# Token-major down projections, and seven block products in place of eight, in a two-layer trunk's MLPs

## The chip, the cores and the metric

One core of a Trainium2 chip runs the whole kernel. The metric is device time in microseconds (us), the median of several executions; lower is better. The engines are TensorE (matrix products; the profile shows its matmuls as PE and its loads of the stationary operand as PEld), VectorE (DVE), ScalarE (ACT), GpSimd (POOL) and SyncE (SP, which issues the loads).

## The reference

256 tokens of width 2048 go through two layers: a gated short convolution with an MLP, then latent attention with an MLP. All is float32. Every sub-layer ends in a layer norm over `alpha * x + f(x)`.

```python
D_MODEL, SEQ, D_FF = 2048, 256, 4 * 2048

def layer_norm(x, g, b):
    mu = jnp.mean(x, axis=-1, keepdims=True)
    var = jnp.mean(jnp.square(x - mu), axis=-1, keepdims=True)
    return (x - mu) * lax.rsqrt(var + LN_EPS) * g + b

def sq_relu_mlp(x, w1, w2):
    return jnp.square(jax.nn.relu(x @ w1)) @ w2

for layer in range(2):
    mix = short_conv_mixer(...) if layer == 0 else mla_mixer(...)
    h = layer_norm(ALPHA * h + mix, ln_g[layer, 0], ln_b[layer, 0])
    h = layer_norm(ALPHA * h + sq_relu_mlp(h, w1[layer], w2[layer]), ln_g[layer, 1], ln_b[layer, 1])
```

Each `w1` is 2048 x 8192 and each `w2` 8192 x 2048: 64 MB each, read once.

## The kernel before, in words

**Layout.** Activations lie with the features on the partitions: `xres` holds 16 chunks of 128 features x 256 tokens. A product has a 128x128 block of weights in the array and streams the tokens.

**Precision.** A float32 value is kept as two parts of type fp32r: `hi`, the value cast to that type, and `lo`, what is left of it. A product of two values takes three partial products: hi·hi, lo·hi and hi·lo. Activations lie as 512 columns, 256 of `hi` and 256 of `lo`, so `high` (line 133) multiplies a weight block's `hi` with all 512 and `low` (line 137) its `lo` with the first 256. This pair is called a **block** here. In a result bank the first 256 columns hold two of the partial sums and the last 256 the third; who reads the bank adds them (`whole`, `residual`). `mm_k1` (lines 151 to 153) makes three 256-wide matmuls of it, so that one sum comes out; `mm_wide` (lines 164 to 166) does the same with 258 columns, which carry the gain and the shift of a layer norm whose statistics come later.

**Weights.** All weights are one `stream` of halves: 128 partitions x 1024 columns, 512 KB. `load` (lines 110 to 113) issues a half's load on SyncE's queue into one of five `raw` buffers, casts it to `hi` on ScalarE (line 112) and makes `lo` on VectorE (line 113), in one of eight pairs of `hi`/`lo` buffers (`whl`). `take` hands out the next halves and lists the conversions of `LOOK` = 4 halves more. Which instruction an engine runs when is fixed by the framework when the kernel is built: it orders each engine's instructions by the order of the listing and by when their inputs and buffers come free. On the chip every engine runs its list in order.

**An MLP.** `mlp` goes through the 8192 hidden features in `NQ` = 8 passes of 1024. In a pass the up part computes 8 chunks of 128 hidden features (16 blocks each); `hidden` adds the partial sums, takes the squared ReLU (VectorE, line 431) and splits the result into `h` (lines 198, 199). The down part then computes, for each of the 16 chunks of output features, 8 blocks over the pass's hidden features, and `residual` adds the two halves of the bank to `xres` (line 354, two 256-wide additions; in the first pass lines 458, 459 with `alpha`). Up and down part have 128 blocks each. In the first pass the up part runs with `mm_wide` and the layer norm before it is applied on the way (`normal`); in the last pass the down part runs with `mm_k1`.

**Behind an MLP.** `Norm.count` sums values and squares over the features as the chunks come out, `stats` turns them into mean and variance through TensorE, and the next stage starts with `widen`/`wide` data. Behind the second MLP, `to_out` scales by the gain, turns the 16 chunks back to tokens on the partitions (line 707), adds mean and shift by a small product of row vectors (line 739), scales by the deviation and stores.

**PSUM.** Eight banks of 512 columns, handed out in turn by `psum`.

Of the kernel before, what the change touches and what calls it, by code (L numbers as in the profile page):

```python
# [15 lines left out]
P = 128  # L16
# [15 lines left out]
LOOK = 4  # L32
RAW, WA = 5, 8
FIRST = ((0, 2, 4, 8), (0, 4, 8))
GROUP = 3
WARM = 8
WO_G = 3
# [5 lines left out]
def trunk(ctx: ExitStack, tc: tile.TileContext, xT, vecs, w_in, w_out, w_kv, w_q, w_uk, w_uv,  # L43
          w_qn, w_qp, w_o, w1, w2, cosT, sinT, mask, ident, gb, out):
# [11 lines left out]
    units = []  # L56
    for m in range(NC):
        units += [w_in[NC + m], w_in[2 * NC + m], w_in[m]]
    units += [w_out[m] for m in range(NC)]

    def mlp_units(l):
        us = []
        for q in range(NQ):
            us += [w1[l, q * QC + m] for m in range(QC)]
            us += [w2[l, m, q] for m in range(NC)]
        return us

    units += mlp_units(0)
    units += [w_kv[m] for m in range(NK + 1)] + [w_q[m] for m in range(NK)]
    for g in range(4):  # L70
        units += [w_uk[g], w_qn[g], w_uv[g], w_qp[g]]
    units += [w_o[m] for m in range(NC)]
    units += mlp_units(1)
    stream = [u[j] for u in units for j in range(u.shape[0])]
# [25 lines left out]
    def load(i, raw=None, cuts=(0, 8)):  # L100

        if raw is None:
            raw = raws.tile([P, 1024], F32, tag="raw", name=f"raw{i}")
        hi = whl.tile([P, 8, P], F32R, tag="hi", name=f"hi{i}")
        lo = whl.tile([P, 8, P], F32R, tag="lo", name=f"lo{i}")
        ready[i] = (hi, lo)
        for b0, b1 in zip(cuts, cuts[1:]):
            at, cols = slice(b0, b1), slice(P * b0, P * b1)
            rv = raw[:, cols].rearrange("p (b c) -> p b c", c=P)
            nc.sync.dma_start(raw[:, cols], stream[i][:, cols])  # L110
            yield
            nc.scalar.copy(hi[:, at, :], rv)  # L112
            nc.vector.tensor_tensor(lo[:, at, :], rv, hi[:, at, :].bitcast(F32), ALU.subtract)  # L113
            yield

    def split_upto(n):
        while state["split"] < min(n, len(stream)):
            for _ in load(state["split"]):
                pass
            state["split"] += 1  # L120

    def take(halves=2):
        i = state["next"]
        state["next"] += halves
        split_upto(i + halves + LOOK)
        return [ready.pop(i + j) for j in range(halves)]
# [12 lines left out]
    def mm_run(wps, x, k0, k1, nk, tiles_first=False):  # L139

        order = [(k, u) for k in range(k0, k1) for u in wps]
        if tiles_first:
            order = [(k, u) for u in wps for k in range(k0, k1)]
        for k, (w, ps) in order:
            high(ps, w, k, x[:, k, :], k == 0)
            low(ps, w, k, x[:, k, :], k == nk - 1)
# [8 lines left out]
    def mm(ps, w, b0, xhl, nk):  # L155

        for k in range(nk):
            mm_k1(ps, w, b0 + k, xhl[:, k, :], k == 0, k == nk - 1)

    def mm_wide(ps, w, xd):  # L160

        for k in range(NC):
            hi, lo = (t[:, k % 8, :] for t in w[k // 8])
            nc.tensor.matmul(ps[:, :W], hi, xd[:, k, :W], start=k == 0, stop=False)  # L164
            nc.tensor.matmul(ps[:, :W], lo, xd[:, k, :W], start=False, stop=False)  # L165
            nc.tensor.matmul(ps[:, :W], hi, xd[:, k, W:], start=False, stop=k == NC - 1)  # L166

    def products(n, x, nk=NC, group=0, cuts=(), halves=True, tiles_first=False):

        ws = [(take(nk // 8), psum("ps_g")) for _ in range(group)]  # L170
        at = [0, *cuts, nk]
        if halves:
            for k0, k1 in zip(at, at[1:]):
                if ws:
                    mm_run(ws, x, k0, k1, nk, tiles_first)
        else:
            for k in range(nk if group else 0):
                for w, ps in ws:
                    mm_k1(ps, w, k, x[:, k, :], k == 0, k == nk - 1)
        yield from [ps for _, ps in ws]  # L180
        for i in range(group, n):
            w = take(nk // 8)
            ps = psum("ps_u")
            if halves:
                mm_run([(w, ps)], x, 0, nk, nk)
            else:
                mm(ps, w, 0, x, nk)
            yield ps

# [32 lines left out]
    def rsqrt(out, ve):  # L222

        s = small.tile([P, 2], F32, tag="sq", name="sq")
        nc.scalar.activation(s, ve, AF.Sqrt)
        iv = small.tile([P, 2], F32, tag="iv", name="iv")
        nc.vector.reciprocal(iv, ve)
        t = small.tile([P, 2], F32, tag="rt", name="rt")
        nc.vector.tensor_tensor(t, s, iv, ALU.mult)
        a = small.tile([P, 2], F32, tag="ra", name="ra")  # L230
# [8 lines left out]
    class Norm:  # L239
# [3 lines left out]
        def __init__(self, idx, scale):  # L243
            self.idx, self.scale, self.hurry = idx, scale, idx == 3
            self.S = act.tile([P, T], F32, tag="S", name=f"S{idx}")
            self.Q = act.tile([P, T], F32, tag="Q", name=f"Q{idx}")
            self.mu0 = act.tile([P, T], F32, tag="mu0", name=f"mu0{idx}")

# [14 lines left out]
        def count(self, m):  # L263
# [7 lines left out]
            if m < NC - 1 or not self.hurry:  # L271
                nc.vector.tensor_tensor(self.S, self.S, d, ALU.add)
                nc.vector.tensor_tensor(self.Q, self.Q, sq, ALU.add)
            else:
                self.last = (d, sq)

        def widen(self):

            self.xd = act.tile([P, NC, 2 * W], F32R, tag="a", name=f"xd{self.idx}")
            v = vec[:, C_G:C_G + 128].rearrange("p (v i m) -> p m i v", v=2, i=4)[:, :, self.idx, :]  # L280
            nc.scalar.copy(self.xd[:, :, T:W], v)
            nc.vector.tensor_tensor(self.xd[:, :, W + T:], v, self.xd[:, :, T:W].bitcast(F32), ALU.subtract)

        def wide(self, m):
            d, x, g = xres[:, m, :], self.xd[:, m, :], self.gain(m)[0]
# [3 lines left out]
        def stats(self):  # L289

            st = psum("stat")
            for j in range(2):
                for b in range(2):
                    c = st[:, 2 * j + b:2 * j + b + 1]
                    tok = slice(b * P, (b + 1) * P)
                    nc.tensor.matmul(c, (self.S, self.Q)[j][:, tok], col[:, 0:1], start=True,
                                     stop=not self.hurry)
                    if self.hurry:
                        nc.tensor.matmul(c, self.last[j][:, tok], col[:, 0:1], start=False, stop=True)
# [7 lines left out]
            return nm, ve, r  # L307

        def finish(self):
            nm, _, r = self.stats()  # L310
# [15 lines left out]
        def normal(self, m, dst=None):  # L326
# [3 lines left out]
            u = tmp.tile([P, T], F32, tag="fh", name="nu")  # L330
# [7 lines left out]
        def weighted(self, ps, f):  # L338
# [6 lines left out]
            nc.scalar.activation(f, t, AF.Identity, bias=v[:, 1:2])  # L345
# [10 lines left out]
    def summed(ln, pss, add, wide):  # L356

        for m, ps in enumerate(pss):
            add(ps, m)
            ln.count(m)  # L360
            wide(m)
# [5 lines left out]
    xhl = act.tile([P, NC, 2 * T], F32R, tag="a", name="xhl0")  # L367

    first = act.tile([P, 2 * GROUP, 1024], F32, tag="b", name="first")
    for half, cuts in enumerate(FIRST):  # L370
        pieces = [load(2 * u + half, first[:, GROUP * half + u, :], cuts) for u in range(GROUP)]
        for b0, b1 in zip(cuts, cuts[1:]):
# [4 lines left out]
            for m in range(at.start, at.stop):  # L377
                put_split(xhl[:, m, :], xres[:, m, :])
# [5 lines left out]
    z = act.tile([P, NC, 2 * T], F32R, tag="b", name="z")  # L384
    cbuf = act.tile([P, 2, 5, T + 2], F32, tag="c", name="cbuf")
    pss = products(3 * NC, xhl, group=GROUP, cuts=(2, 4, 8, 12), tiles_first=True)
    ln = Norm(0, ALPHA)
    for m in range(NC):
        parts = []
        for what in "cub":  # L390
# [3 lines left out]
            parts.append(f)  # L394
            if what == "u":
                v = cbuf[:, m % 2, 3, :]
                nc.gpsimd.memset(v[:, 0:2], 0.0)
                nc.vector.tensor_tensor(v[:, 2:], parts[0], parts[1], ALU.mult)
# [5 lines left out]
        nc.vector.tensor_tensor(y, y, parts[2], ALU.mult)  # L404
        put_split(z[:, m, :], y)
# [4 lines left out]
    ln.widen()  # L410
    summed(ln, products(NC, z), residual, ln.wide)

    def mlp(idx, ln, last):

        xhl = act.tile([P, NC, 2 * T], F32R, tag="b", name=f"xhl{idx}")
        todo = iter(range(NC))

        def normal():
            k = next(todo, None)
            if k is not None:  # L420
                ln.normal(k, xhl[:, k, :])

        for q in range(NQ):
            h = act.tile([P, QC, 2 * T], F32R, tag="c", name=f"h{idx}_{q}")
            if q == NQ - 1:
                ln = Norm(idx, None)

            def hidden(m, ps, evac):
                f = tmp.tile([P, T], F32, tag="fh", name="fh")
                evac(ps, f)  # L430
                nc.vector.scalar_tensor_tensor(f, f, 0.0, f, ALU.max, ALU.mult)  # L431
                put_split(h[:, m, :], f)

            if q == 0:
                for m in range(QC):
                    w = take()
                    ps = psum("ps_w")
                    mm_wide(ps, w, ln.xd)
                    if m == 0:
                        ln.finish()  # L440
                    hidden(m, ps, ln.weighted)
                    if m > 0:
                        normal()
            else:
                for m, ps in enumerate(products(QC, xhl)):
                    hidden(m, ps, whole)
                    if q == NQ - 1:
                        for k in range(2 * m, 2 * m + 2):
                            ln.prepare(k)
            if q == NQ - 1:  # L450
                last(ln, products(NC, h, QC, 2, halves=False))
                return ln
            pss = products(NC, h, QC, 2, (6,))
            for m, ps in enumerate(pss):
                if q == 0:
                    normal()
                    d = xres[:, m, :]
                    nc.vector.scalar_tensor_tensor(d, d, ALPHA, ps[:, T:], ALU.mult, ALU.add)
                    nc.vector.tensor_tensor(d, d, ps[:, :T], ALU.add)
                else:  # L460
                    residual(ps, m)

    def to_wide(ln, pss):
        ln.widen()
# [352 lines left out]
```

## Time and profile before

| | us |
|---|---|
| median of 3 runs | 2079.16 (2077.47 to 2081.31) |
| the profiled execution | 2080.19 |
| its span, first to last instruction | 2078.4 |
| granted TensorE clock, mean | 0.998 |
| passes of the MLPs in the trace, one of the six alike | 88.7 |
| last product of the kernel ends | 2063.4 |
| loads of weights | 512 KB each, 4.1 from issue to landing for those of the MLPs |
| bytes read | 379.20 MB, 183 GB/s over the span |

A row of the costliest groups reads: line, engine, operation, what is written and read by the program's names, shapes, number of instructions | time in which at least one of them ran, mean nanoseconds of one | idle time of the engine ahead of them, and who ended most of it. Matmuls overlap, so a matmul's duration is longer than the time until the next one starts. A row of the timeline reads: start, time covered, engine, line, operation, shapes, number of instructions merged into the row, and in brackets idle time ahead of it with what ended it.

### The profile page before, as it was taken

What the parts mean: (1) busy time and instruction counts of PE and PEld (TensorE: products, weight loads), DVE (VectorE), ACT (ScalarE), POOL (GpSimd) and SP (SyncE); (2) the same over time, 40 slices, a digit from 0 to 9 for tenths busy, and PEclk for the clock granted to TensorE, in tenths of its full rate; (3) what the DMA queues carried; (4) which work ended last, traced back from release to release, by engine and by line L of the source; (5) the groups of instructions that cost most, each with busy time, mean ns of one, the idle gap of its engine ahead of it and who ended that gap; (6) DMA issues with size and microseconds to landing.
All of it is one profiled execution on the core that took longest, in us unless ns stands there. A gap on an engine that the chain in (4) does not pass through costs nothing.

```text
span 2078.4 us, 32534 instructions
## 1 busy us (share of the span) xinstructions
PE 2068.4 (100%) x12640; PEld 1841.6 (89%) x12640; DVE 1512.2 (73%) x2490; ACT 1010.8 (49%) x1473; POOL 2.2 (0%) x21
## 2 busy tenths in 40 slices
PE   9999999999999999999999999999999999999998
PEld 8888888988888888888899998898888888888898
DVE  7667677886676767667788878788667676676776
ACT  6444445654444443444456665565444444444354
POOL 0000000000000000000000000000000000000000
PEclk9999999999999999999999999999999999999999
DMA  8555555555555556565555444556555555555551
GB/s 312 196 186 189 190 185 188 176 193 187 191 191 193 188 179 202 190 189 190 192 183 173 133 142 143 188 167 202 190 188 190 193 190 187 192 192 190 188 183 62
DMA packets 107447, 383.42 MB, mean 184 GB/s; under 512 B 11927, under 2 KB 13335, under 8 KB 107287
## 3 DMA queue, kind: packets, MB, share of 16 engines
q1 hardware_dynamic: 107148, 381.09, 56.1%
q8 instruction: 99, 1.62, 0.3%
q14 instruction: 56, 0.45, 0.1%
q10 hardware_dynamic: 144, 0.26, 0.0%
HBM read 379.20 MB, written 2.10 MB: 183 GB/s over the span
## 4 chain that ended last, share of the span: by engine, by line
PE 98%; DVE 1%; DMA 0%; ACT 0%; issue 0%; DVEq 0%; ACTq 0%
PE ps_u L133 51%; PE ps_u L137 25%; PE ps_g L133 3%; PE ps_w L166 2%; PE ps_w L164 2%; PE ps_w L165 2%; PE ps_g L137 1%; PE ps_u L152 1%; PE ps_u L151 1%; PE ps_u L153 1%; PE S L612 0%; DMA xres<-in_xT_dram 0%; PE S L611 0%; PE ps_q L153 0%; PE ps_q L152 0%; PE ps_q L151 0%
## 5 line engine op out<-in xcount | busy, mean ns | idle before, releaser
L112 ACT CAST hi<-raw 128x1024 fp32r<-128x1024 f32 x712 | 747.7, 1053 | 909.1 <-PE ps_u L133 775.6
L113 DVE TENSOR_TENSOR lo<-raw,hi 128x1024 fp32r<-128x1024 f32 x712 | 870.4, 1224 | 366.6 <-ACT hi L112 344.0
L133 PE MATMUL ps_u<-xhl,hi 128*128 128x512 f32 x2512 | 874.8, 394 | 0.0
L137 PE MATMUL ps_u<-xhl,lo 128*128 128x256 f32 x2512 | 698.0, 278 | 0.0
L133 PEld LDWEIGHTS ps_u<-xhl,hi 128*128 128x128 f32 x2512 | 471.1, 188 | 110.1
L133 PE MATMUL ps_u<-h,hi 128*128 128x512 f32 x1568 | 544.2, 394 | 0.0
L137 PEld LDWEIGHTS ps_u<-xhl,lo 128*128 128x128 f32 x2512 | 472.2, 188 | 0.1
L137 PE MATMUL ps_u<-h,lo 128*128 128x256 f32 x1568 | 434.3, 277 | 0.0
L133 PEld LDWEIGHTS ps_u<-h,hi 128*128 128x128 f32 x1568 | 294.0, 188 | 68.3
L137 PEld LDWEIGHTS ps_u<-h,lo 128*128 128x128 f32 x1568 | 294.3, 188 | 0.0
L354 DVE TENSOR_TENSOR xres<-xres,ps_u 128x256 f32<-128x256 f32 x422 | 177.2, 420 | 116.2 <-PE ps_u L137 99.9
L166 PE MATMUL ps_w<-xd,hi 128*128 128x258 f32 x400 | 113.3, 284 | 0.0
L164 PE MATMUL ps_w<-xd,hi 128*128 128x258 f32 x400 | 113.2, 283 | 0.0
L165 PE MATMUL ps_w<-xd,lo 128*128 128x258 f32 x400 | 112.9, 282 | 0.0
L133 PE MATMUL ps_u<-z,hi 128*128 128x512 f32 x256 | 90.6, 399 | 0.0
L133 PE MATMUL ps_g<-h,hi 128*128 128x512 f32 x224 | 78.3, 394 | 0.0
L164 PEld LDWEIGHTS ps_w<-xd,hi 128*128 128x128 f32 x400 | 76.3, 191 | 0.1
L166 PEld LDWEIGHTS ps_w<-xd,hi 128*128 128x128 f32 x400 | 75.7, 190 | 0.0
L165 PEld LDWEIGHTS ps_w<-xd,lo 128*128 128x128 f32 x400 | 75.2, 188 | 0.0
L133 PE MATMUL ps_u<-oT,hi 128*128 128x512 f32 x208 | 73.5, 399 | 0.0
L137 PE MATMUL ps_u<-z,lo 128*128 128x256 f32 x256 | 71.7, 281 | 0.0
L198 ACT CAST h<-fh 128x256 fp32r<-128x256 f32 x128 | 51.5, 402 | 36.6 <-DVE fh L431 36.6
(211 smaller groups left out, 2091.2 us busy)
## 6 DMA issues: line engine op xcount, KB each, us to landing
raw<-in_w_dram SPq DMA_DIRECT2D x512, 512.0 KB, 4.1
raw<-in_w_in_dram SPq DMA_DIRECT2D x90, 512.0 KB, 3.4
raw<-in_w_out_dram SPq DMA_DIRECT2D x32, 512.0 KB, 3.3
raw<-in_w_o_dram SPq DMA_DIRECT2D x32, 512.0 KB, 3.4
raw<-in_w_kv_dram SPq DMA_DIRECT2D x10, 512.0 KB, 4.2
raw<-in_w_q_dram SPq DMA_DIRECT2D x8, 512.0 KB, 3.4
raw<-in_w_uk_dram SPq DMA_DIRECT2D x8, 512.0 KB, 3.3
raw<-in_w_qn_dram SPq DMA_DIRECT2D x8, 512.0 KB, 3.3
```

The lines of the kernel that those rows point to most:

```text
L112: nc.scalar.copy(hi[:, at, :], rv)
L113: nc.vector.tensor_tensor(lo[:, at, :], rv, hi[:, at, :].bitcast(F32), ALU.subtract)
L133: nc.tensor.matmul(ps, w[blk // 8][0][:, blk % 8, :], x, start=first, stop=False)
L137: nc.tensor.matmul(ps[:, :T], w[blk // 8][1][:, blk % 8, :], x[:, :T], start=False, stop=last)
L151: nc.tensor.matmul(ps[:, :T], lo, x[:, :T], start=first, stop=False)
L152: nc.tensor.matmul(ps[:, :T], hi, x[:, T:], start=False, stop=False)
L153: nc.tensor.matmul(ps[:, :T], hi, x[:, :T], start=False, stop=last)
L164: nc.tensor.matmul(ps[:, :W], hi, xd[:, k, :W], start=k == 0, stop=False)
L165: nc.tensor.matmul(ps[:, :W], lo, xd[:, k, :W], start=False, stop=False)
L166: nc.tensor.matmul(ps[:, :W], hi, xd[:, k, W:], start=False, stop=k == NC - 1)
L198: nc.scalar.copy(dst[:, :T], src)
L354: nc.vector.tensor_tensor(d, d, ps[:, :T], ALU.add)
```

## The change

All down projections of both MLPs change sides: the split activations stay in the array (128 hidden features x 128 tokens), and 512 columns of weights stream (`dot`, three matmuls of 512: hi·hi, hi·lo, lo·hi). A result bank then holds 128 tokens x 512 output features, complete; `put` adds it to a new accumulator `acc` (two token halves x 2048). A plain down projection goes through four column blocks `n` of 512 (`down`), each with two token halves `t` and 8 hidden chunks: 64 dots a pass.

In the six passes `FAST` = 1 to 6 of each MLP, the first two column blocks come from `down_fast`. For each pair of hidden chunks (1 and 2) the two token halves, the two hidden chunks and the two column blocks make a 2x2 by 2x2 product of blocks, which is done with seven products in place of eight, by sums and differences of the blocks (Strassen's scheme in Winograd's form). Four pairs make 28 dots instead of 32. The seven results stay in seven banks over the four pairs and are merged into `acc` behind them. The sums of the weight blocks are made in `prepare` on VectorE from two raw halves and converted (one unit: three pairs of hi/lo buffers, and a buffer of its own, `t4`, for the fourth difference); those of the activations in `hidden`.

At the end of the first MLP the accumulator is turned back to features on the partitions with 32 transposes, and the next stage's first three wide products run around the last of them. At the end of the second MLP the residual is turned to tokens first, and the last norm is taken along the free axis. `LOOK` becomes 5, with a unit counted as 3. The squared ReLU goes to ScalarE as a ReLU and a square. Large tiles are cut in two (`a1`, `a2`) and buffers `fh` become three.

```diff
-LOOK = 4
+LOOK = 5
+NB = 4
+BW = D // NB
+FAST = range(1, NQ - 1)
+TAIL = 4
...
+    def prepare(i):
+        if len(stream[i]) == 1:
+            raw = load_raw(i, stream[i][0])
+            hi, lo = ready[i] = parts(i)
+            split(hi, lo, tiled(raw))
+            return
+        r1, r2 = (load_raw(f"{i}_{j}", src) for j, src in enumerate(stream[i]))
+        out = []
+        def finished(r, name):
+            hi, lo = parts(name)
+            split(hi, lo, tiled(r))
+            out.append((hi, lo))
+        b22, (b21, b12) = r1[:, BW:], (r2[:, :BW], r2[:, BW:])
+        finished(r1, f"{i}_1")
+        t = raws.tile([P, 1024], F32, tag="raw", name=f"raw{i}_t")
+        two = "p (a c) -> p a c"
+        nc.vector.tensor_tensor(t.rearrange(two, a=2), b12.unsqueeze(1).to_broadcast([P, 2, BW]),
+                                r1.rearrange(two, a=2), ALU.subtract)
+        finished(t, f"{i}_t")
+        nc.vector.tensor_tensor(b12, b22, t[:, :BW], ALU.subtract)
+        finished(r2, f"{i}_2")
+        t4 = r1[:, :BW]
+        nc.vector.tensor_tensor(t4, b21, b12, ALU.subtract)
+        f = state["fast"].tile([P, 2, BW], F32R, tag="t4", name=f"t4_{i}")
+        split(f[:, 0, :], f[:, 1, :], t4)
...
+    def size(i):
+        return 1 if len(stream[i]) == 1 else 3
     def take(halves=2):
         i = state["next"]
         state["next"] += halves
-        split_upto(i + halves + LOOK)
+        ahead = -sum(size(j) for j in range(i, i + halves))
+        for j in range(i, len(stream)):
+            ahead += size(j)
+            if ahead > LOOK:
+                break
+            if j >= state["split"]:
+                prepare(j)
+                state["split"] = j + 1
...
+    def dot(ps, w, x, first, last):
+        nc.tensor.matmul(ps, x[0], w[0], start=first, stop=False)
+        nc.tensor.matmul(ps, x[0], w[1], start=False, stop=False)
+        nc.tensor.matmul(ps, x[1], w[0], start=False, stop=last)
...
+    FACTORS = (("4", "22", "T4"), ("2", "12", "21"), ("3", "S4", "22"), ("1", "11", "11"),
+               ("6", "S2", "T2"), ("7", "S3", "T3"), ("5", "S1", "T1"))
+    def down_fast(x, forms):
+        ps = {p: psum(f"ps_f{p}") for p, _, _ in FACTORS}
+        n = len(x) // 2
+        for j in range(n):
+            b, = take(1)
+            a = {"11": held(x[2 * j], 0), "12": held(x[2 * j + 1], 0), "22": held(x[2 * j + 1], 1)}
+            for i in range(4):
+                a[f"S{i + 1}"] = [forms[:, j, o, i * P:(i + 1) * P] for o in range(2)]
+            for p, l, r in FACTORS:
+                dot(ps[p], b[r], a[l], j == 0, j == n - 1)
+        return ps
...
+                if not func:
+                    nc.scalar.activation(f, f, AF.Relu)
+                nc.scalar.activation(f, f, AF.Square)
+                put_split(h[m], f)
...
+                    nc.vector.tensor_tensor(s1, a21, a22, ALU.add)
+                    nc.vector.tensor_tensor(s3, a21, a11, ALU.subtract)
+                    nc.vector.tensor_tensor(s2, s1, a11, ALU.subtract)
+                    nc.vector.tensor_tensor(s4, a12, s2, ALU.subtract)
+                    split(forms[:, m // 2, 0, :], forms[:, m // 2, 1, :], sf.rearrange("p i c -> p (i c)"))
...
+            def put(n, t, ps):
+                if q == 0:
+                    nc.scalar.copy(block(n, t), ps)
+                    for _ in range(2):
+                        normal()
+                else:
+                    nc.vector.tensor_tensor(block(n, t), block(n, t), ps, ALU.add)
...
+            if q in FAST:
+                p = down_fast(h, forms)
+                put(0, 1, p["4"])
+                put(0, 0, p["2"])
+                put(1, 0, p["3"])
+                v, u = (raws.tile([P, 2, BW], F32, tag="raw", name="vu")[:, i, :] for i in range(2))
+                put(0, 0, p["1"])
+                nc.scalar.copy(v, p["1"])
+                nc.vector.tensor_tensor(v, v, p["6"], ALU.add)
+                nc.vector.tensor_tensor(u, v, p["7"], ALU.add)
+                put(1, 0, v)
+                put(0, 1, u)
+                put(1, 0, p["5"])
+                put(1, 1, u)
+                put(1, 1, p["5"])
+            for n in range(2 if q in FAST else 0, NB):
+                down(h, put, n)
...
+    def to_wide(block, put, down):
+        def turned(n):
+            for c in range(2):
+                ps = psum("turned")
+                for j in range(4):
+                    src = block(n, j % 2)[:, (2 * c + j // 2) * P:(2 * c + j // 2 + 1) * P]
+                    nc.tensor.transpose(ps[:, j * P:(j + 1) * P], src, id_t)
+                summed(ln, [ps[:, j * T:(j + 1) * T] for j in range(2)], add, 4 * n + 2 * c)
+        ln.widen("b")
+        for n in range(NB):
+            down(put, n)
+            if n:
+                turned(n - 1)
+        ln.ws = group_of(GROUP)
+        mm_wide(ln.ws, ln.xd, 0, NC - 4)
+        turned(NB - 1)
+        mm_wide(ln.ws, ln.xd, NC - 4)
...
+    def to_out(block, put, down):
+        gbt = act.tile([P, NB, 2 * BW], F32, tag="b", name="gbt")
+        for n in range(NB):
+            nc.gpsimd.dma_start(gbt[:, n, :], gb[n].partition_broadcast(P))
...
+        def finished(n, t, ps):
+            put(n, t, ps)
+            nc.vector.bn_stats(out=stats[:, t, n, :], in_=block(n, t))
+            if n < NB - 1:
+                return
...
+            rsqrt(r, ve)
+            for i in range(NB):
+                d, u = block(i, t), raws.tile([P, 1024], F32, tag="raw", name="u")[:, :BW]
+                nc.vector.scalar_tensor_tensor(u, d, mv[:, 0:1], gbt[:, i, :BW], ALU.subtract, ALU.mult)
+                nc.vector.scalar_tensor_tensor(d, u, r, gbt[:, i, BW:], ALU.mult, ALU.add)
+                nc.sync.dma_start(out[t * P:(t + 1) * P, i * BW:(i + 1) * BW], d)
+        for n in range(NB):
+            down(finished, n, TAIL if n == NB - 1 else 0)
```

On the host, `w2` is laid out as rows of 512 columns for two hidden chunks to a half, and once more (`w2f`) in the order of the pairs for the fast passes; each weight is still loaded once.

423 lines of the change are left out of this document (206 added, 217 removed).

## The prediction

> **What bounds the kernel now.** I read the page from the top: busy shares, then the chain that ended last, then the costliest groups; then the waits, one pass by itself, and single instructions where the change needs a price.
>
> ```profile
> PE 2068.4 (100%) x12640; PEld 1841.6 (89%) x12640; DVE 1512.2 (73%) x2490; ACT 1010.8 (49%) x1473; POOL 2.2 (0%) x21
> ...
> PE 98%; DVE 1%; DMA 0%; ACT 0%; issue 0%; DVEq 0%; ACTq 0%
> ...
> L112 ACT CAST hi<-raw 128x1024 fp32r<-128x1024 f32 x712 | 747.7, 1053 | 909.1 <-PE ps_u L133 775.6
> L113 DVE TENSOR_TENSOR lo<-raw,hi 128x1024 fp32r<-128x1024 f32 x712 | 870.4, 1224 | 366.6 <-ACT hi L112 344.0
> L133 PE MATMUL ps_u<-xhl,hi 128*128 128x512 f32 x2512 | 874.8, 394 | 0.0
> L137 PE MATMUL ps_u<-xhl,lo 128*128 128x256 f32 x2512 | 698.0, 278 | 0.0
> ```
>
> TensorE is the bound: 98% of the chain, and no idle time before its groups. VectorE has a quarter of the span free. What ScalarE's casts wait for (775.6 us) is TensorE giving back converted weights: the conversion runs as far ahead as the eight hi/lo buffers let it, although the listing asks for four halves (LOOK). Counting both sequences, a half in the fourth pass is converted 17 us before its first use. So the order of the listing is a priority, not the order on the engines.
>
> One pass of the first MLP, of the six that look alike:
>
> ```profile
> core 0: us, PE busy (x) PEld busy (x) DVE busy (x) ACT busy (x) POOL busy (x), PEclk, DMA share, GB/s
> ...
> 549.50:638.20 88.70, 88.70 (x513) 77.55 (x513) 60.88 (x89) 38.30 (x48) 0.00 (x0) 1.00 0.59 190
> ```
>
> TensorE is full for 88.7 us, VectorE works 60.9 of them. A pass is 256 blocks (128 up, 128 down), so a block, one 512-wide and one 256-wide matmul, costs 0.3465 us.
>
> **The price of the new form.** The new products hold the activations in the array and stream 512 weight columns, three matmuls to a product. The attention's value projection already does just that (lines 590 to 592; start, duration):
>
> ```profile
> 1149.40 0.40 PE L590 MATMUL ps_v<-hi,lat 128*128 128x512 f32 x1
> 1149.64 0.39 PE L591 MATMUL ps_v<-lo,lat 128*128 128x512 f32 x1
> 1149.87 0.39 PE L592 MATMUL ps_v<-hi,lat 128*128 128x512 f32 x1
> 1150.10 0.39 PE L590 MATMUL ps_v<-hi,lat 128*128 128x512 f32 x1
> 1150.32 0.39 PE L591 MATMUL ps_v<-lo,lat 128*128 128x512 f32 x1
> 1150.55 0.39 PE L592 MATMUL ps_v<-hi,lat 128*128 128x512 f32 x1
> 1150.78 0.39 PE L590 MATMUL ps_v<-hi,lat 128*128 128x512 f32 x1
> ```
>
> Starts, not durations, are the price, since matmuls overlap: six in 1.38 us, 0.230 each; later ones of the run come every 0.227. A product costs 0.680 to 0.690; I take 0.685. It replaces two blocks, 0.693. The upper bound for the same work is 0.696, twice the sum of the median spacings of the block's two forms in the whole trace (0.231 and 0.117).
>
> **TensorE's part of the sum.**
> - A down projection is 64 such products, or 28 + 32 = 60 in the twelve fast passes. Before, 128 x 0.3465 = 44.35 us; fast, 60 x 0.685 = 41.10. Saved 3.25 x 12 = 39.0.
> - The two first passes keep 64 products: 43.84, saved 0.5 x 2 = 1.0.
> - The two last passes ran three 256-wide matmuls a block (lines 151 to 153, started every 0.120 us): 128 x 0.361 = 46.2. Now 43.84, saved 2.4 x 2 = 4.7.
> - The first MLP's result now lies with tokens on the partitions and is turned back: 32 transposes at 0.108 us (the start spacing of line 707's): +3.5. The second MLP's 32 replace 32.
> - Together -41.2. With 0.680 a product it is -46, with 0.696 -30.
>
> **The end.** Before, the last product ended at 2063.4 and the span at 2078.4: 15 us of statistics, row products, scaling and stores. After, the last token half does an addition (0.69), statistics of 512 elements (about 0.7), some eight small operations (0.16 to 0.20 each in this tail), four pairs of 512-wide operations and a store (2.4 us from issue to landing): about 11 us, behind the first token half's same work, of which some 2 us stick out behind the 5.5 us of its last products. 13 us, -2. Bounds: -5 if nothing sticks out and the store is short, +4 if the first half's work comes wholly first.
>
> **VectorE's and ScalarE's part.** What one 1024-wide conversion costs here is in the groups above, and the 512-wide row of the start gives the half size:
>
> ```profile
> 18.22 1.90 DVE L113 TENSOR_TENSOR lo<-first,hi 128x512 fp32r<-128x512 f32 x3
> ...
> 616.05 1.23 DVE L113 TENSOR_TENSOR lo<-raw,hi 128x1024 fp32r<-128x1024 f32 x1
> 617.81 0.88 DVE L354 TENSOR_TENSOR xres<-xres,ps_u 128x256 f32<-128x256 f32 x2 [0.54 <-PE ps_u L137]
> ```
>
> Three 512-wide take 1.90 us with 0.69 for the last: one starts each 0.60. Likewise 1.14 for 1024 (median spacing of line 113's when another follows), 0.34 for 256 independent and 0.45 dependent; 128 worked out as 0.20 to 0.31.
> A fast unit (one pair of loads, seven products, 7 x 0.685 = 4.8 us of TensorE) needs on VectorE three low parts and one 1024-wide difference, 4 x 1.14, and two 512-wide differences and a low part, 3 x 0.60: 6.36 us. ScalarE: 3 x 1.05 + 0.62 = 3.8, below TensorE's. So **inside the fast stage VectorE is slower than TensorE by 1.5 us a unit**, four units long. New too: the sums of the activations, 1.6 us to each of four pairs, and eleven 512-wide additions where the seven results are merged (6.6 us), instead of 16 of 256 (line 354). The square of the ReLU goes to ScalarE.
> A whole fast pass for VectorE: 24 plain halves 27.4, four units 25.4, hidden tiles 8 x 0.8, sums 6.4, fifteen additions 9: 74.6 us out of 44.35 + 41.1 = 85.5. Over a pass it fits; the question is how far ahead it can get before the stage.
>
> Ledger of the stage, 0 being the first product of the first unit. Eight hi/lo pairs: while the last up chunk holds two, three belong to unit 0 and three to unit 1. The up stage leaves VectorE idle (10 halves 11.4, seven hidden tiles and three sums 10.4, units 0 and 1 12.1: 34 of 44), so at 0 both are converted, all but unit 1's T4, whose one buffer is free when the first product of unit 0 has ended (0.9). From 0.5 VectorE has: last hidden tile 0.8, last sums 1.6, T4 of unit 1 0.6, and of unit 2 what is left behind its first low part, 5.2: ready at 8.7, wanted at 9.6. Unit 3 takes 6.36 more: 15.1, wanted at 14.4. **Late by 0.7**. The casts between (1.05) and the one T4 buffer make it wait in places where nothing else is ready; I take 1.5 us a pass, **+18 in all**. Lower bound 0, since TensorE can't run ahead of its rows. Upper bound: only one unit is ahead, unit 1 is ready at 0.5 + 2.4 + 6.36 = 9.3, unit 3 two units later at 22.0 instead of 14.4: 7.6 a pass, +91.
> While ScalarE's cast of T4 waits for TensorE, the casts behind it on ScalarE wait, and for these VectorE's low parts: that is how a small delay of T4 can become one of a whole unit.
> Behind the stage the first plain product needs two banks, and the second is that of product 4, whose addition may stand behind five conversions (5.7 us): 15.1 + 5.7 + 0.6 = 21.4 against 20.0 + 0.7. It is covered by loads that land later than that, or costs 0.7 a pass; within the 1.5.
> What is left costs nothing: the three wide units taken together run the same matmuls; the first passes' additions become ScalarE copies of 0.62 in an engine half idle; the four broadcast loads of gains go out on POOL's queue, which issues little else, some 40 us ahead of their use, and would cost their landing (about 4 us) at the end if they came late.
> Loads: the same bytes, eight halves in 20 us at the stage, some 210 GB/s against the 190 of a pass now at a DMA share of 0.59. Nothing, and if raw buffers (five, three to a unit) come free late, it is the upper bound above.
>
> By the Trainium skill, page "VectorE: DVE Perf Modes", section Terms, every operation of the engine drains its pipe before the next may issue, which speaks against an edit that adds so many. By that rule an operation would cost its whole duration, and the sum would be that of the second rival. The trace disagrees where operations are independent: 0.60 between starts for a duration of 0.69.
>
> **Sum.** The profiled execution took 2080.19 (span 2078.4 and 1.8 around it), 1.0 above the median of 2079.16. 2079.2 - 41.2 - 2 + 18 = **2054**.
>
> **Rivals.**
> 1. *TensorE alone decides.* The conversion keeps up, and the product costs 0.680 to 0.690: 2079 - 43 = 2036, down to 2031 with 0.680. For it: 12% of VectorE left in the pass. Against: 6.36 over 4.8 in the stage.
> 2. *Full durations.* 6.96 a unit (4 x 1.224 + 3 x 0.688), and unit 3 is late by about 2.3 instead of 0.7: 12 x 2.3 = 28, 2064. Against: the spacing above.
> 3. *Slower: one unit ahead.* LOOK of 5 lists one unit of size 3, five raw buffers hold two, T4 one; if the engines' fixed order keeps to that, each unit waits for VectorE. It decides from 43 / 12 = 3.6 us a pass. At the bound 2036 + 91 = 2127; at half way between 3.6 and 7.6, 2036 + 67 = 2103. Against: conversions that today run 17 us ahead.
> 4. *Even.* The stall is 3.3 to 3.9 us a pass, 2075 to 2083.
>
> **Chances.** Forecast 0.42 (its own range 2044 to 2072), rival 1 0.13, 2 0.07, 3 0.30, 4 0.08. Under 0.2%, some 4 us, a measurement of this kernel can't tell a change from none (its three runs span 3.8 us). Faster 0.62, same 0.08, slower 0.30. The range goes from 2034 to 2112: of rival 1 the lower third and of rival 3 the upper third stay outside, about 0.14.
>
> **What would show it.** The page: about 11,240 matmuls instead of 12,640, DVE near 85%, PE idle of 10 to 30 us in all, in front of the products with T4. A fast pass 85 to 88.7 us long. Starts of the new products 0.227 to 0.232 apart. If units 1, 2 and 3 each begin with a wait on T4's low part of 2 us or more, rival 3 holds; if a product costs over 0.70, the first term is wrong.

## The result, and the profile after

The changed kernel takes **2055.84 us** (median of 4 runs, 2055.07 to 2056.39) against 2078.31 for the kernel before in the same comparison: a ratio of 0.9884, 95% interval 0.9872 to 0.9896. The forecast was 2054 and faster. The profiled execution took 2055.07 us with a span of 2053.3; 2080.19 and 2078.4 before, so 25.1 us went.

The page, busy shares, chain by engine, then groups:

```profile
PE 2033.1 (99%) x11220; PEld 1761.9 (86%) x11220; DVE 1638.2 (80%) x2555; ACT 1184.8 (58%) x1847; POOL 4.5 (0%) x25
...
PE 97%; DVE 2%; DMA 0%; issue 0%; ACT 0%; DVEq 0%
...
L113 DVE TENSOR_TENSOR lo<-raw,hi 128x1024 fp32r<-128x1024 f32 x712 | 862.2, 1222 | 315.1 <-ACT hi L112 310.5
L112 ACT CAST hi<-raw 128x1024 fp32r<-128x1024 f32 x712 | 742.0, 1049 | 538.5 <-PE ps_u L191 295.3
...
L248 PE MATMUL ps_d<-hi,h 128*128 128x512 f32 x640 | 249.3, 390 | 0.0
```

TensorE is still the bound, with 1420 matmuls fewer; VectorE went from 73% to 80% of the span, not to the 85% forecast (in the fast pass below it is busy for 74.9 of 86.5 us). The third pass of the first MLP, up part, the stage of the seven products, and the plain down products; columns as before:

```profile
547.26:592.47 45.21, 45.21 (x258) 39.23 (x256) 38.06 (x59) 29.17 (x49) 0.00 (x0) 1.00 0.54 175
592.47:612.00 19.53, 19.53 (x87) 15.86 (x86) 18.07 (x24) 13.10 (x18) 0.00 (x0) 1.00 0.57 181
612.00:633.77 21.77, 21.77 (x97) 17.98 (x96) 18.81 (x23) 10.73 (x12) 0.00 (x0) 1.00 0.76 262
```

TensorE has no idle time in any of them. The pass is 86.5 us instead of 88.75. The down part is 41.3 us instead of 44.4. **The up part, whose matmuls nobody touched, is 45.2 instead of 44.4.** That is the first surprise. The second is that the wait forecast in the stage does not exist, though VectorE is full there (18.07 of 19.53):

```profile
586.95 1.22 DVE L155 TENSOR_TENSOR raw_t<-raw,raw 128x1024 f32<-128x1024 f32 x1
...
590.56 0.68 DVE L158 TENSOR_TENSOR raw<-raw,raw_t 128x512 f32<-128x512 f32 x1
...
592.95 0.69 DVE L161 TENSOR_TENSOR raw<-raw 128x512 f32<-128x512 f32 x1
593.63 1.23 DVE L113 TENSOR_TENSOR lo_t<-raw_t,hi_t 128x1024 fp32r<-128x1024 f32 x1
594.77 0.42 DVE L301 TENSOR_TENSOR fh<-ps_u,t 128x256 f32<-128x256 f32 x1
595.11 0.68 DVE L113 TENSOR_TENSOR t<-raw,t 128x512 fp32r<-128x512 f32 x1
...
599.46 0.68 DVE L113 TENSOR_TENSOR t<-raw,t 128x512 fp32r<-128x512 f32 x1
...
605.80 0.68 DVE L113 TENSOR_TENSOR t<-raw,t 128x512 fp32r<-128x512 f32 x1
```

The rows `t<-raw,t` are the low parts of T4, the last piece of units 1, 2 and 3. They end at 595.8, 600.1 and 606.5. The stage began at 592.47 and TensorE needs a unit each 4.88 us, at 597.35, 602.2 and 607.1. So VectorE is ahead by 1.5, 2.1 and **0.6 us**; over all twelve passes the smallest lead at unit 3 is 0.60. The first two rows shown are the 1024-wide difference of unit 2 and its first 512-wide one, both done before the stage begins.

Where the 25.1 us come from, stage by stage (differences of the starts of the stages' first matmuls in the two traces):

| | us |
|---|---|
| twelve fast down parts, 44.37 to 41.31 | -36.8 |
| twelve up parts of the same passes, 44.37 to 45.21 | +10.1 |
| two first down parts, 44.4 to 43.55 | -1.7 |
| last down parts with their transposes | -1.0 |
| attention up to its output projection, of it 2.85 in one wait (experiment e8) | +4.6 |
| its output projection, 73.5 to 72.1 | -1.4 |
| end, 14.9 to 13.5 | -1.4 |
| rest (start, convolution, first and last up parts) | +2.4 |

### The profile page after: what moved, and what is told of

The parts are those of the page before. It is cut to its first block, busy times and chain, and to the rows that moved or that the text cites. A ratio compares the mean times of both kernels' runs of the same rounds, so it can differ in the third digit from the quotient of the medians.

```text
span 2053.3 us, 30156 instructions
## 1 busy us (share of the span) xinstructions
PE 2033.1 (99%) x11220; PEld 1761.9 (86%) x11220; DVE 1638.2 (80%) x2555; ACT 1184.8 (58%) x1847; POOL 4.5 (0%) x25
## 4 chain that ended last, share of the span: by engine, by line
PE 97%; DVE 2%; DMA 0%; issue 0%; ACT 0%; DVEq 0%
PE ps_u L191 34%; PE ps_u L195 17%; PE ps_d L250 7%; PE ps_d L249 7%; PE ps_d L248 7%; PE ps_f L250 4%; PE ps_f L248 4%; PE ps_f L249 4%; PE ps_w L225 1%; PE ps_w L223 1%; PE ps_w L224 1%; PE ps_g L223 1%; PE ps_g L225 1%; PE ps_g L224 1%; PE ps_wo L191 1%; PE S L781 1%
## 5 line engine op out<-in xcount | busy, mean ns | idle before, releaser
L191 PE MATMUL ps_u<-xhl,hi 128*128 128x512 f32 x1792 | 632.9, 398 | 0.0
L195 PE MATMUL ps_u<-xhl,lo 128*128 128x256 f32 x1792 | 503.1, 281 | 0.0
L191 PEld LDWEIGHTS ps_u<-xhl,hi 128*128 128x128 f32 x1792 | 336.6, 188 | 83.1
L191 PE MATMUL ps_u<-xhl_a,hi 128*128 128x512 f32 x720 | 253.5, 396 | 0.0
L248 PE MATMUL ps_d<-hi,h 128*128 128x512 f32 x640 | 249.3, 390 | 0.0
L250 PE MATMUL ps_d<-hi,h 128*128 128x512 f32 x640 | 249.3, 390 | 0.0
L249 PE MATMUL ps_d<-lo,h 128*128 128x512 f32 x640 | 249.2, 389 | 0.0
L195 PE MATMUL ps_u<-xhl_a,lo 128*128 128x256 f32 x720 | 203.0, 282 | 0.0
L191 PEld LDWEIGHTS ps_u<-xhl_a,hi 128*128 128x128 f32 x720 | 135.3, 188 | 32.0
L248 PEld LDWEIGHTS ps_d<-hi,h 128*128 128x128 f32 x640 | 120.2, 188 | 25.2
L250 PEld LDWEIGHTS ps_d<-hi,h 128*128 128x128 f32 x640 | 120.1, 188 | 25.0
L195 PEld LDWEIGHTS ps_u<-xhl_a,lo 128*128 128x128 f32 x720 | 135.8, 189 | 0.0
L191 PE MATMUL ps_u<-z,hi 128*128 128x512 f32 x256 | 90.6, 399 | 0.0
```

The source lines that it names most:

```text
L191: nc.tensor.matmul(ps, w[blk // 8][0][:, blk % 8, :], x, start=first, stop=False)
L195: nc.tensor.matmul(ps[:, :T], w[blk // 8][1][:, blk % 8, :], x[:, :T], start=False, stop=last)
L248: nc.tensor.matmul(ps, x[0], w[0], start=first, stop=False)
L249: nc.tensor.matmul(ps, x[0], w[1], start=False, stop=False)
L250: nc.tensor.matmul(ps, x[1], w[0], start=False, stop=last)
```

## Experiments

Each is an edit of the changed kernel unless said. Ratios are to the kernel before in the same comparison, with the 95% interval.

**e1_plain: the form without the seven products.**

```diff
-FAST = range(1, NQ - 1)
+FAST = range(0)
```

> All down projections as plain products, 64 to a pass, no pass with seven. Compared with the changed kernel (2055.8 us) each of twelve passes has four more products, 43.5 instead of 41.3 us for its down part. Theory A (the up blocks' slower rhythm, 0.3533 us a block instead of 0.3467, is set by the products that run before them): up stages stay at 45.2 us, time 2055.8 + 12 x 2.25 = 2083 us. Theory B (it comes from VectorE's and ScalarE's added work in the pass): up stages go back to 44.4 us, time 2073 us. If the stage of the seven products hid a wait, the time falls below both.

Measured: 2081.0 us, ratio 1.0006 (0.9996 to 1.0015). All twelve up parts stay at 45.21 us although VectorE has nothing new to do in them (it is busy for 23.8 us of a stretch of 45, against 27.8 in the kernel before and 34.7 in the changed one); the down parts are 43.58. Theory B falls for VectorE. ScalarE keeps its added square here, so for ScalarE it falls only with e6 below. And the new form alone is worth nothing: 0.8 us a pass won in the down part, 0.84 lost in the up part. The gain of the change is that of the seven products.

**e2_nudge, e3_swap, e6_mu: disturbing the entry of the up part.** The edits, in this order:

```diff
+                if q in FAST:
+                    nc.tensor.matmul(psum("nudge")[:, :P], ones, ones, start=True, stop=True)
                 for m, ps in enumerate(products(QC, xhl)):
```

```diff
+            if swap and k == 1:
+                low(ps, w, k, x[k], False)
+                high(ps, w, k, x[k], False)
+                continue
             high(ps, w, k, x[k], k == 0)
...
-                for m, ps in enumerate(products(QC, xhl)):
+                for m, ps in enumerate(products(QC, xhl, swap=q in FAST)):
```

```diff
+                if q in FAST:
+                    nc.tensor.matmul(psum("nudge")[:, :T], ones, xres[:, 0, :], start=True, stop=True)
                 for m, ps in enumerate(products(QC, xhl)):
```

> The changed kernel with one 128x128 float32 matmul of ones into a bank of its own ahead of the up part of each of the twelve fast passes. Theory A (rhythm by entry): the up stages fall from 45.2 to 44.4 us, less about 0.2 us for the added matmul, 2055.8 - 12 x 0.6 = 2048 us. Theory B (load on SBUF by the other engines): up stages stay at 45.2 us, 2058 us.

> The changed kernel with the two matmuls of the second block of each fast pass's up part in the other order, no work added. Theory A: one disturbance at the entry is enough to move the whole stage into the other rhythm, 45.2 to 44.4 us, 2046 us; it may also stay if this disturbance is not of the right size. Theory B: 2056 us.

> The changed kernel with one 256-wide float32 matmul (of the kind that the norm's first mean uses, 0.43 us) into a bank of its own ahead of the up part of each of the twelve fast passes. In the last passes, where such a matmul stands there anyway, the up part runs at 0.3467 us a block. Theory A (rhythm by entry, of the right kind): up stages 45.2 to 44.4 us, together with the added matmul 2055 - 12 x 0.4 = 2050 us. If the entry is not it, up stages stay at 45.2 and the time is 2060 us.

Measured: e2 2057.2 us, ratio 0.9889 (0.9874 to 0.9903), up parts 45.30; e3 2055.92, 0.9887 (0.9872 to 0.9902), up parts 45.20. In neither does the rhythm change; e2 pays for its added matmuls. **e6: 2050.2 us, 0.9853 (0.9838 to 0.9868)**, and all twelve up parts take 44.57. The entry in the changed kernel, from its timeline, and in e6:

```profile
547.03 0.39 PE L250 MATMUL ps_d<-hi,h 128*128 128x512 f32 x1
547.26 0.39 PE L191 MATMUL ps_u<-xhl,hi 128*128 128x512 f32 x1
547.48 0.28 PE L195 MATMUL ps_u<-xhl,lo 128*128 128x256 f32 x1
547.60 0.40 PE L191 MATMUL ps_u<-xhl,hi 128*128 128x512 f32 x1
547.83 0.28 PE L195 MATMUL ps_u<-xhl,lo 128*128 128x256 f32 x1
547.95 0.40 PE L191 MATMUL ps_u<-xhl,hi 128*128 128x512 f32 x1
548.19 0.28 PE L195 MATMUL ps_u<-xhl,lo 128*128 128x256 f32 x1
548.31 0.40 PE L191 MATMUL ps_u<-xhl,hi 128*128 128x512 f32 x1
```

```profile
547.07 0.59 PE L580 MATMUL nudge<-xres,ones 128*128 128x256 f32 x2
547.31 0.59 PE L191 MATMUL ps_u<-xhl,hi 128*128 128x512 f32 x1
547.74 0.28 PE L195 MATMUL ps_u<-xhl,lo 128*128 128x256 f32 x1
547.86 0.39 PE L191 MATMUL ps_u<-xhl,hi 128*128 128x512 f32 x1
548.09 0.28 PE L195 MATMUL ps_u<-xhl,lo 128*128 128x256 f32 x1
548.20 0.39 PE L191 MATMUL ps_u<-xhl,hi 128*128 128x512 f32 x1
548.43 0.28 PE L195 MATMUL ps_u<-xhl,lo 128*128 128x256 f32 x1
548.55 0.39 PE L191 MATMUL ps_u<-xhl,hi 128*128 128x512 f32 x1
```

Read the starts of the 512-wide rows. In the changed kernel they come every 0.35 to 0.36 us, in e6 every 0.34 to 0.35. To the nanosecond, the spacings in the changed kernel repeat as 113, 233, 117, 241, 120, 236 (1060 for three blocks, 353.3 each), in e6 as 230, 117, 230, 117, 230, 116 (1040, 346.7 each). The instructions of the stage and their data are the same. The added matmul takes a result bank, so the stage's banks move on by one; in e2 they do so too, without effect. The rhythm that is taken at the entry lasts here for the 256 matmuls of the stage. The two profiled executions are 4.9 us apart (the medians 5.6). Of these 3.7 lie in the twelve passes, 0.3 each: 0.64 won in the up part, the rest paid at the added matmul and behind it. Another 1.3 lie ahead of the attention's output projection, where one wait is 0.68 instead of 2.85 in this build and other places are longer. e6 is the fastest version run; its interval against the kernel before lies below the changed kernel's.

**e10_more_mu, e11_before_mu: more such entries, and in the kernel before.** e10 adds the same matmul ahead of the second MLP's last up part and of the convolution's output projection; e11 puts it into the kernel before, ahead of the two output projections (shown):

```diff
+    def nudge():
+        nc.tensor.matmul(psum("nudge")[:, :T], ones, xres[:, 0, :], start=True, stop=True)
...
+    nudge()
     summed(ln, products(NC, z), residual, ln.wide)
...
+        nudge()
         yield from products(NC - WO_G, oT)
```

> The changed kernel with the 256-wide float32 matmul ahead of the up parts of all passes but the first, and ahead of the convolution's output projection. Theory A (entry sets the rhythm): the second MLP's last up part falls from 45.2 to 44.6 us and the output projection from 90.6 to 89.0, so 2050.2 - 0.2 - 1.2 = 2049 us. If the output projection does not follow, 2050 us.

> The kernel before, with such a matmul ahead of the convolution's output projection (90.6 us there) and of the attention's (73.5 us, 0.3533 us a block). Theory A: 89.0 and 72.1 us, 2079 - 1.6 - 1.4 + 0.9 = 2077 us. Rival: in that kernel the rhythm has another cause, stages unchanged, 2080 us.

Measured: e10 2052.62 us, 0.9868 (0.9854 to 0.9881): the last up part falls to 44.57 as expected, the convolution's output projection stays at 90.64, and the attention's, which nothing was put ahead of, goes from 72.1 to 73.5, 1.4 of the 2.6 us above the expected 2050. e11 2079.87 us, 0.9998 (0.9989 to 1.0007): the convolution's output projection falls from 90.58 to 88.94, and the attention's runs at 346.7 ns a pair instead of 353.3, though the time is at the rival's number and can't be told from that of the kernel before. Only the attention's stage is switched at its entry. The convolution's stage in the kernel before begins at 346.7 anyway; it changes to 353.3 at its 16th block (282.3 us), where TensorE has to wait a moment for the last chunk of its input `z`, and two 512-wide matmuls follow each other. With the added matmul the stage starts 0.8 us later, and this place is gone. So both rhythms occur in both kernels, and an added matmul can switch them, but the same one does it in one place and not in another.

**e4_t_twice, e12_t_three, e7_t_four: more VectorE work in each unit.** The 1024-wide difference is made two, three or four times:

```diff
-        nc.vector.tensor_tensor(t.rearrange(two, a=2), b12.unsqueeze(1).to_broadcast([P, 2, BW]),
-                                r1.rearrange(two, a=2), ALU.subtract)
+        for _ in range(2):
+            nc.vector.tensor_tensor(t.rearrange(two, a=2), b12.unsqueeze(1).to_broadcast([P, 2, BW]),
+                                    r1.rearrange(two, a=2), ALU.subtract)
```

> The changed kernel with the 1024-wide difference of every fast unit made twice: 1.14 us more of VectorE to a unit, nothing else. Theory C (the conversion keeps just ahead: by the trace the low part of T4 of unit 3 is there 0.6 us before its use, of unit 1 1.5 and of unit 2 2.1): unit 3 comes late by 1.7 to 2.8 us in every fast pass, 2076 to 2090 us, with the wait in front of the products with T4. Rival D (VectorE has room, the conversions move ahead into the up stage): 2056 to 2061 us.

> The changed kernel with the 1024-wide difference of every fast unit made four times: 3.4 us more of VectorE to a unit, 13.7 to a fast pass, which then has about 88 us of VectorE against 86.5 of TensorE. Theory F (room over the whole pass decides, since conversions and products both move): a fast pass becomes VectorE's 88 to 90 us, 2055 + 12 x 1.5 to 3.5 = 2073 to 2097 us. Theory C (the stage decides): unit 2 and 3 late by about 8 us together in every fast pass, 2140 us and more.

> The changed kernel with the 1024-wide difference of every fast unit made three times: 9.1 us more of VectorE to a fast pass. Two times (4.6 us) cost 2 us in all, four times (13.7 us) 122 us, 10.1 a pass. Theory G (a fast pass absorbs about 4 us of VectorE by running conversions ahead and ready products first, and what goes beyond comes out in full): 9.1 - 4 = 5 us a pass, 2055 + 60 = 2115 us. Rival F (only the sum over the pass counts, 83.7 us of VectorE under 86.5 of TensorE): 2056 to 2062 us.

| | VectorE added to a pass | time, us | ratio (95%) | cost of a pass |
|---|---|---|---|---|
| changed | 0 | 2055.84 | 0.9884 (0.9872 to 0.9896) | |
| e4 | 4 x 1.14 = 4.6 | 2058.0 | 0.9892 (0.9877 to 0.9907) | 2.2 / 12 = 0.2 |
| e12 | 9.1 | 2109.19 | 1.0138 (1.0124 to 1.0152) | 53.4 / 12 = 4.4 |
| e7 | 13.7 | 2177.76 | 1.0468 (1.045 to 1.0485) | 121.9 / 12 = 10.2 |

The last column divides the whole difference by twelve; of the profiled executions' differences 1.4, 52.4 and 116.5 us lie in the twelve passes (0.1, 4.4 and 9.7 each). About 4.5 to 5.5 us more a pass are absorbed, and what goes beyond comes out nearly in full. e7 fits theory C's 2140 us and more, e12 is 6 us below theory G's 2115. Rival F, the sum over the pass, falls: in e12 a pass has 83.3 to 83.6 us of VectorE and TensorE waits all the same. e4 comes out at rival D's number, but not in its way, since the conversions don't move ahead: the low part of T4 of unit 0 is there 12.5 us before the stage in most passes, against 13 in the changed kernel. In e4 the low part of T4 of unit 3 comes 2.3 us after the unit's first product, as theory C had it, and yet TensorE does not wait. Its order is another; VectorE's row for this low part, and TensorE's for unit 3 of the same pass:

```profile
608.35 0.69 DVE L113 TENSOR_TENSOR t<-raw,t 128x512 fp32r<-128x512 f32 x1
```

```profile
606.76 0.39 PE L249 MATMUL ps_f<-hi,forms 128*128 128x512 f32 x1
607.00 0.39 PE L250 MATMUL ps_f<-lo,forms 128*128 128x512 f32 x1
...
607.69 0.39 PE L249 MATMUL ps_f<-t,h 128*128 128x512 f32 x1
...
609.55 0.40 PE L250 MATMUL ps_f<-t,h 128*128 128x512 f32 x1
```

The unit starts with another product and reaches T4's low part (the row at 609.55, after the operation that ended at 609.04) in the middle. The framework had laid out TensorE's list that way when the kernel was built. In e7 the stage and the plain products behind it last 50.67 us with a granted clock of 0.93, against 41.31 at 1.00: part of the cost there is the clock. It is at 0.5 for 3.4 or 6.8 us in each of e7's twelve fast passes, and for 3.4 us in seven of e12's, there within 2 us behind waits of TensorE of 2.3 to 2.7 us; in e12's other five the same waits don't lower it. Matmuls then start 427 ns apart instead of 232, which by their number is an estimated 1.1 us a pass in e7 and 0.7 in e12.

**e5_six: six hi/lo pairs.**

```diff
-RAW, WA = 5, 8
+RAW, WA = 5, 6
```

> The changed kernel with six hi/lo pairs instead of eight, so that no second unit can be converted before TensorE starts the first. Theory C (the pairs are what lets VectorE get ahead): unit 1 comes late by about 4 us and units 2 and 3 again, up to the 7.6 us a fast pass of the record's third rival, 2055 + 40 to 91 = 2095 to 2146 us. Theory E (what gets ahead is the differences, which need raw buffers only, and TensorE takes ready products first): below 2 us a pass, 2055 to 2080 us.

Measured: 2069.3 us, 0.9945 (0.9931 to 0.996): 13.5 us above the changed kernel. The two profiled executions are 11.3 apart, and of these 6.5 lie in the twelve passes, 0.5 each. Another 6.6 lie between the last fast pass of the first MLP and the attention's output projection, where the wait that e8 is about is longer (4.4 us idle against 2.7) and the clock is at 0.5 for 6.8 us behind it; the convolution's output projection is 1.5 faster. In the median of the twelve passes unit 1's T4 is there 0.5 us ahead (1.5 in the changed kernel), those of units 2 and 3 come 2.6 and 3.7 us behind the start that these units have there, and TensorE's list begins these units with other products. Theory C falls by its number, theory E holds; two pairs fewer cost something, not 4 us a pass.

**e8_rk_later: the attention's wait.**

```diff
-            if m == 0:
+            if m == 1:
                 rms(rc, csq)
-            if m == 1:
+            if m == 2:
                 rkp = psum("rkp")
```

> The changed kernel with the attention's key scale taken from its sum one chunk later (statistics behind the second query chunk, spreading behind the third). The trace has TensorE wait 2.85 us for it there, because VectorE's queue is behind. Theory: the wait goes, 2055 - 2.5 = 2052 to 2053 us. Rival: VectorE's lateness shows at the next point, 2055 us.

Measured: 2056.17 us, 0.9882 (0.9867 to 0.9897). The rival holds by its number: the wait of 2.85 us (from start to start; 2.69 by the profile's idle time) is gone, but TensorE now waits 0.4, 0.9 and 1.2 us at the layer norm's spreading some 20 us earlier, and behind it the granted clock of the stretch is 0.79 (0.5 for 3.4 us, from 1099.9 to 1103.3).

```profile
1096.00:1104.00 8.00, 6.12 (x35) 5.64 (x36) 7.62 (x19) 5.66 (x14) 0.00 (x0) 0.79 0.81 284
```

VectorE is busy for 7.62 of these 8 us, as it is in the changed kernel; where the small operations stand in its queue differs from build to build. Of e8's time 1.4 us are something else: the attention's output projection runs in the slower rhythm here (73.5 us against 72.1).

**e9_order: products 1 and 6 exchanged.**

```diff
-    FACTORS = (("4", "22", "T4"), ("2", "12", "21"), ("3", "S4", "22"), ("1", "11", "11"),
-               ("6", "S2", "T2"), ("7", "S3", "T3"), ("5", "S1", "T1"))
+    FACTORS = (("4", "22", "T4"), ("2", "12", "21"), ("3", "S4", "22"), ("6", "S2", "T2"),
+               ("1", "11", "11"), ("7", "S3", "T3"), ("5", "S1", "T1"))
```

> The changed kernel with products 1 and 6 of the seven exchanged in order (4, 2, 3, 6, 1, 7, 5). The trace has the matmuls of the seven products 0.232 us apart on average against 0.227 in the plain ones, the slow ones (0.233 to 0.241) always at the same places of the unit. If a product's operands make it slow, the slow places move with product 6; if it is the rhythm of the issue, they stay or change as a whole. The time stays at 2055 us either way, at most 5 us less if all become 0.227.

Measured: 2055.6 us (one run). The mean spacing stays at 0.232. The slow places (0.241) move, from matmuls 13, 20 and 21 of the 21 of a unit to 9 and 16, which are not those of product 6. So there is no sign that product 6 is slow by its operands. Why seven different products run 0.232 apart and the plain ones 0.227 is open.

## Why the prediction was right, point by point

**The direction and the sum.** 2054 forecast, 2055.84 measured. That the sum comes out this close is luck. The stall of 18 us isn't there. Against it stand 10.1 in the up parts and 5.6 in the attention and the table's last row, for none of which there was a term, and 2.3 less saved in the down parts and at the end.

**TensorE's down parts: right.** 60 products at 0.685 were to make 41.10 us; it is 41.31. The plain products run at 0.227 (32 x 0.681 = 21.8), the lower price; the seven at 0.232 (28 x 0.696 = 19.5), the upper bound taken from the blocks. Saved 36.8 against 39.0. The two first down parts gave 1.7 against 1.0.

**"Late by 0.7 ... I take 1.5 us a pass, +18 in all": wrong, it is 0.** The ledger's order of VectorE's work was the failing step. It let only unit 2's first low part be made before the stage begins. The trace has unit 2's 1024-wide difference done 4.3 us before it and its first 512-wide one 1.2 us, 1.7 us of work that the ledger had in the stage: by the code the differences need only raw buffers, and no hi/lo pair. So unit 3 is ready at 14.0 us, wanted at 14.6, where the ledger had 15.1 and 14.4. And a T4 that is late by 2.3 us need not be a wait either (e4): the list is then laid out with another product first. The margin is small, 0.6 us by the trace and about 5 us of VectorE a pass by e4, e12 and e7, so that the lower bound held, but not by much.

**"Nothing" for the up part: wrong, it is +10.1.** No term stood for it. e1 shows that it is not VectorE's load, and e6 that 0.64 of the 0.84 us a stage go when the stage is entered in another way, with the other engines' work as it was.

**The end.** 1.4 us won against 2. The additional transposes are inside the last down parts' row.

**The rivals.** TensorE alone (2036): there is no wait in the stage, as it says, but it priced the up part by the row of before. Full durations: behind a low part of 512, which lasts 0.68 us, the next independent operation starts after 0.60 in the new trace too (599.46 to 600.06). So the rule of the Trainium skill, page "VectorE: DVE Perf Modes", section Terms, that the next operation waits for the pipe to empty, does not hold here for independent operations. One unit ahead: e5 is the nearest to it, and costs 0.5 us a pass, not 3.6 to 7.6; with three times the difference (e12) the change is slower than before, by a mechanism close to the rival's, since units 2 and 3 wait for VectorE there, though unit 1 doesn't. That the range reached to 2112 was more than needed.

**Marks given beforehand.** 11,220 matmuls against 11,240; VectorE 80% against 85%; no idle time of TensorE in the stages of the seven products, and so no wait on T4; new products 0.227 to 0.232 apart, as said; a fast pass 86.5 us, within 85 to 88.7.

## What to carry to other kernels

When an engine is full for one stage only, count what it can do before the stage begins by the buffers that each piece needs, piece by piece, and look whether the waiting engine's list can be rearranged; then find the margin by doubling one piece, for behind it nearly every microsecond comes out (0.2, 4.4 and 10.2 us a pass for 4.6, 9.1 and 13.7 added). When neighbouring code is exchanged, price the untouched stages again: the spacing of identical matmuls may change with what runs ahead of them. A change that saves products in a kernel that TensorE bounds is worth what the starts of the matmuls say, not their number.

## What the runs showed of the hardware that was not expected

The same stream of matmuls (512 and 256 columns in turn) runs at 346.7 or 353.3 ns a pair, at a granted clock of 1.00, without any idle time in the profile, and keeps its rhythm until something disturbs it, for 256 matmuls and more. The changed kernel's convolution products show a third, uneven one of 352 on average (135.0 us for 384 pairs).

One 256-wide float32 matmul ahead of a stage set the rhythm anew. Behind the down products of the new form, which start 227 ns apart, the pairs ran at 346.7 every time (twelve stages in e6, thirteen in e10, and the first MLP's last up part in the changed kernel, where the layer norm has such a matmul). Behind the convolution's uneven products in e10 they ran at 353.3. A 128-wide one (e2) and two matmuls exchanged (e3) left 353.3. In the kernel before, the up parts follow down products of the same two widths, which run at 346.7 already.

Stages that no edit touches differ between builds: the convolution's output projection took 90.6 us in the changed kernel and 89.0 in e4, e5 and e9, the attention's 72.1 in the changed kernel and 73.5 in e1, e8, e9 and e10. In the first of the two the place can be seen. All builds of the changed kernel but e10 enter it at 353 and have the wait for `z` at its 16th block; behind that wait e4, e5 and e9 run at 346.7 and the others at 353.3, while the pause itself differs by 2 ns at most (301 to 303 from the first 512-wide matmul to the second). What selects the rhythm stays open. In a kernel that is all matmuls it moves about 2% of a stage, so differences of a few microseconds between builds need a look at the spacing before they are given a cause.
